# Asking for one packet per load and engine: a packet setting on the row-group loads of a load-bound prefix-sum kernel

## The chip, the cores and the metric

The kernel runs on one core of one Trainium2 chip. The metric is the device time of one execution in microseconds (us), as the median of several runs. The kernel before takes 669.56 us (three runs, 668.67 to 670.19).

## The reference

```python
# x: float32 [4, 4224, 4224]
ps = np.cumsum(np.cumsum(x, axis=1), axis=2)
diag = np.diagonal(ps, axis1=1, axis2=2)
return np.cumsum(diag, axis=1)            # float32 [4, 4224]
```

Every element of `x` counts for some diagonal entry, so all 285 MB have to be read. The rest is adding up.

## The kernel before

A *strip* is six rows for each of the 128 partitions, 768 rows by 4224 columns. It is loaded by one transfer issued from POOL, which casts f32 to bf16 on the way. Three strip buffers rotate. TensorE adds up column groups, VectorE (DVE) and ScalarE add up row parts, and a short chain of small operations ends each of the four batches.

```python
NBUF = 3
strips = ctx.enter_context(tc.tile_pool(name="strips", bufs=NBUF))
...
def strip_tile():
    return strips.tile([P, F2, N], BF16, name="strip")      # 128 x 6 x 4224

def load_rows(o, b, r0):
    f = o.shape[1]
    nc.gpsimd.dma_start(
        out=o, in_=x[b, r0 : r0 + f * P, :].rearrange("(p f) w -> p f w", f=f)
    )

prefetched = []
for i in range(NBUF):
    t = strip_tile()
    load_rows(t, 0, i * F2 * P)
    prefetched.append(t)
...
for b in range(B):
    ...
    for s in range(ns):
        strip = prefetched.pop(0) if prefetched else None
        if strip is None:
            strip = strip_tile()                 # waits until the oldest strip is used up
            load_rows(strip, b, s * F2 * P)
        add_up(strip, F2, s * F2 * P, acc6[:, s], um6)
    ...                                          # a three-row strip, then the batch's end
    nc.sync.dma_start(out=out[b, : j1 * GW]...)  # small stores, on the SP queue
```

The corner of the last batch is loaded by a few smaller transfers that do not go through `load_rows`; the change does not touch them.

Of the kernel before, what the change touches and what calls it, by code (L numbers as in the profile page):

```python
# [17 lines left out]
def kernel(  # L18
# [17 lines left out]
    P = 128  # L36
# [36 lines left out]
    def load_rows(o, b, r0):  # L73
        f = o.shape[1]
        nc.gpsimd.dma_start(  # L75
            out=o, in_=x[b, r0 : r0 + f * P, :].rearrange("(p f) w -> p f w", f=f)
        )

    prefetched = []
# [4 lines that stand above are left out]
# [6 lines left out]
    def upper_mask(f):  # L90
# [20 lines left out]
        out=um1,  # L111
        in_=um1,
# [10 lines left out]
        out=ident,  # L123
        in_=ident,
# [32 lines left out]
    def between_groups(name, turned):  # L157
# [27 lines left out]
        out=weights,  # L185
        in_=weights,
# [61 lines left out]
    for h in range(2):  # L248
        w = GW - h * P
# [3 lines left out]
    for b in range(B):  # L253
# [55 lines left out]
# [3 lines that stand above are left out]
                strip = strip_tile()  # L312
                load_rows(strip, b, s * F2 * P)
            add_up(strip, F2, s * F2 * P, acc6[:, s], um6)
            if not whole and s == 0:
                diag_b = last.tile([P, P], BF16, name="diag_b")
                nc.gpsimd.dma_start(out=diag_b, in_=x[b, TB:N, TB:N])
            if not whole and s == 1:
                row_sums(hs[:, 2:3], diag_b)
                masked(hmu[:, 2, :P], diag_b, um1[:, :P], hu[:, 2:3])  # L320
                nc.vector.tensor_sub(
                    out=tsum[:, 0:1], in0=hs[:, 2:3], in1=hu[:, 2:3]
                )
                for h in range(3):
                    columns(LG, h * P, GW, hmu[:, h, : GW - h * P])
        a6 = acc6[:, :ns]
        sum_up(a6)
        for h in range(2):
# [3 lines left out]
                out=r6[ps, k : k + 2 * ns : 2, :], in_=a6[ps, :, :, 1]  # L332
# [3 lines left out]
        if whole:  # L336
            load_rows(strip[:, :F], b, T0)
            add_up(strip[:, :F], F, T0, acc3[:, 0], um3)
            sum_up(acc3[:, 0])
            nc.vector.tensor_copy(out=r3[:, LG, :], in_=acc3[:, 0, :, 1])  # L340
        else:


            for h in range(2):
                load_rows(strip[:, h * F : h * F + F], b, T0 - (2 - h) * GW)
            add_up(strip[:, :F], F, T0 - 2 * GW, acc3[:, 0], um3)
            sum_up(acc3[:, 0])
            nc.vector.tensor_copy(out=r3[:, row_of(LG - 2), :], in_=acc3[:, 0, :, 1])
            fold_g = psum_s.tile([P, F, 160], FP32, name="fold")
            wp, ws = 1280, 1280 + 1536  # L350
            fold_in(fold_g, strip[:, F:], 0, wp, 160, start=True)
            parts = last.tile([P, F, 4], FP32, name="parts")
            add_up(strip[:, F:], F, T0 - GW, parts, um3, wp, ws)
            nc.vector.tensor_scalar_mul(
                out=parts[:, :, 2], in0=parts[:, :, 2], scalar1=-1.0
            )
            row_sums(parts[:, :, 3], fold_g)
            row_sums(r3[:, row_of(LG - 1), :], parts)
# [37 lines left out]
        for i, src in enumerate((d, c12[:, 0, :])):  # L396
            nc.vector.tensor_tensor_scan(  # L397
                out=c12[:, i, :],
# [8 lines left out]
            out=out[b, : j1 * GW].rearrange("(g i) -> g i", i=GW),  # L407
            in_=c12[t0:NG, 1, :],
# [36 lines left out]
        for fin, c0, c1 in ((fin_a, 0, 2 * P), (fin_b, 2 * P, GW)):  # L445
            nc.vector.tensor_add(
                out=yl[:, c0:c1], in0=fin, in1=c12[0:1, 1, c0:c1]
            )
            nc.sync.dma_start(
                out=out[b, T0 + c0 : T0 + c1].unsqueeze(0), in_=yl[:, c0:c1]  # L450
# [31 lines left out]
```

## Time and profile before

| what | value | where from |
|---|---|---|
| span of the profiled run | 667.0 us | first line of the page |
| DMA engines | nine tenths or more in 39 of 40 slices | slices |
| TensorE / DVE / ScalarE busy | 32% / 50% / 21% | busy times |
| one six-row load, issue to landing | 69.6 us (median) | DMA issues |
| same load, landing to landing | 29.9 us | chain of waits |

The last two rows belong together. A load takes 29.9 us of the engines' time, and the 69.6 us from issue to landing say that it stands in a queue for some 40 us first. A queue that is never empty is what bounds this kernel. The lines themselves are in the prediction.

### The profile page before, as it was taken

To read this page: it belongs to the slowest core of one execution; us is meant where nothing else is said; L and a number is where in the kernel's file an instruction comes from. 1 tells how busy PE (TensorE), PEld (TensorE's weight loads), DVE (VectorE), ACT (ScalarE), POOL (GpSimd) and SP (SyncE) were. 2 spreads that over 40 slices of the span, in tenths; PEclk is the share of its full clock that TensorE was granted. 3 is DMA by queue.
4 is the path that set the end of the run, shared out by engine and by line. 5 is a ranking of instruction groups with operands and counts; after the bars stand their busy time and mean duration, and the time that the engine had idled before them with its cause. 6 is when DMAs were issued, how large, how long until landed. Compare 5 with 4: busy or idle time off the path is not lost.

```text
span 667.0 us, 2828 instructions
## 1 busy us (share of the span) xinstructions
PE 215.1 (32%) x967; PEld 97.2 (15%) x967; DVE 336.3 (50%) x376; ACT 140.1 (21%) x225; POOL 27.0 (4%) x56
## 2 busy tenths in 40 slices
PE   0071522403118254140321633504032254250426
PEld 0030211101003022010110311201011122120202
DVE  2043617366924351745883415266398241635687
ACT  0001120406300103040630020304063002030436
POOL 5000000000000000000000000000000000001000
PEclk9995857666558586665655957567565586765758
DMA  9999999999999999999999999999999999999997
GB/s 203 219 219 219 218 219 219 217 217 216 208 215 219 219 219 217 216 219 219 219 219 215 216 211 217 220 219 216 216 216 219 220 215 218 216 215 219 216 207 144
DMA packets 7384, 143.25 MB, mean 215 GB/s; under 512 B 669, under 2 KB 842, under 8 KB 1866
## 3 DMA queue, kind: packets, MB, share of 16 engines
q0 software_dynamic: 7008, 142.47, 99.7%
q1 hardware_dynamic: 362, 0.61, 0.3%
q8 instruction: 7, 0.11, 0.1%
q14 instruction: 7, 0.06, 0.0%
HBM read 285.47 MB, written 0.07 MB: 428 GB/s over the span
## 4 chain that ended last, share of the span: by engine, by line
another core or an unknown queue 42%; DVE 25%; PE 23%; DMA 5%; issue 4%; DVEq 0%; POOLq 0%
PE d L198 23%; DVE acc L215 17%; DVE mu L218 7%; DMA strip<-in_x_dram 5%; PE fold L198 1%; DVE pu L215 0%; DVE c L397 0%; DVE c L218 0%; DVE tsum L215 0%; DVE acc L301 0%; DVE acc L304 0%; PE carry_ps L198 0%; DVE rows L331 0%; DVEq L218 0%
## 5 line engine op out<-in xcount | busy, mean ns | idle before, releaser
L218 DVE SCALAR_TENSOR_TENSOR mu<-strip,um 128x768 bf16<-128x768 bf16 (+1 forms) x129 | 110.7, 908 | 314.4 <-DMA strip<-in_x_dram 222.3
L198 PE MATMUL d<-strip,sel 128*11 128x384 bf16 x603 | 140.0, 406 | 344.4 <-DMA strip<-in_x_dram 344.4
L210 ACT ACTIVATE dump<-strip 128x416 bf16<-128x416 bf16 (+8 forms) x112 | 128.4, 1146 | 523.2 <-DMA strip<-in_x_dram 520.2
L215 DVE TENSOR_REDUCE acc<-strip 128x6 f32<-128x4608 bf16 (+6 forms) x23 | 195.9, 8518 | 0.0
L198 PEld LDWEIGHTS <-sel 128*11 128x11 bf16 x849 | 86.1, 101 | 526.3 <-issue 488.4
L198 PE MATMUL d<-mu,sel 128*11 128x384 bf16 x243 | 59.7, 355 | 67.5 <-DVE mu L218 67.4
L75 POOL DMA_DIRECT2D strip<-in_x_dram x24 | 16.5, 687 | 555.5 <-DVE acc L215 414.5
L210 ACT ACTIVATION_READ_ACCUMULATOR dump<-strip 128x1 f32 x112 | 20.9, 186 | 0.0
L218 DVE DVE_READ_ACCUMULATOR mu<-strip,um 128x1 f32 x129 | 10.6, 82 | 0.0
L198 PE MATMUL d<-ident,rows 128*11 128x128 f32 x24 | 5.2, 378 | 16.5 <-DVE rows L340 16.5
L198 PE MATMUL fold<-strip,ident_h 128*128 128x480 bf16 (+1 forms) x14 | 4.3, 458 | 8.4 <-DMA strip<-in_x_dram 8.4
L198 PE MATMUL d<-halves,rows 128*11 128x64 f32 x48 | 5.7, 304 | 0.0
L198 PEld LDWEIGHTS d<-halves,rows 128*11 128x11 f32 x48 | 5.1, 136 | 2.1 <-issue 2.1
L198 PEld LDWEIGHTS d<-ident,rows 128*11 128x11 f32 x24 | 2.6, 118 | 18.2 <-DVE rows L340 11.5
L215 DVE TENSOR_REDUCE pu<-d 11x1 f32<-11x384 f32 x4 | 2.2, 546 | 5.5 <-PE d L198 5.5
L397 DVE TENSOR_TENSOR_SCAN c<-ones_row,carry,c 11x384 f32<-11x384 f32 x4 | 4.0, 1006 | 0.1
L397 DVE TENSOR_TENSOR_SCAN c<-ones_row,carry,d 11x384 f32<-11x384 f32 x4 | 4.0, 1001 | 0.1
L198 PEld LDWEIGHTS <-ident_h 128*128 128x128 bf16 x20 | 2.2, 112 | 12.2 <-issue 11.8
L215 DVE TENSOR_REDUCE parts<-strip 128x3 f32<-128x3072 bf16 x1 | 3.4, 3350 | 0.0
L198 PE MATMUL d<-hmu,sel 128*11 128x384 bf16 (+2 forms) x3 | 0.7, 286 | 6.7 <-DVE hmu L218 6.7
L372 POOL DMA_DIRECT2D strip<-in_x_dram x2 | 1.4, 716 | 29.2 <-DVE acc L215 29.2
L215 DVE TENSOR_REDUCE tsum<-strip 128x1 f32<-128x384 bf16 (+2 forms) x3 | 1.7, 568 | 0.9 <-DMA strip<-in_x_dram 0.9
(78 smaller groups left out, 36.0 us busy)
## 6 DMA issues: line engine op xcount, KB each, us to landing
strip<-in_x_dram POOLq DMA_DIRECT2D x19, 6336.0 KB, 69.6
strip<-in_x_dram POOLq DMA_DIRECT2D x5, 3168.0 KB, 55.3
strip<-in_x_dram POOLq DMA_DIRECT2D x1, 1080.0 KB, 45.3
strip<-in_x_dram POOLq DMA_DIRECT2D x1, 768.0 KB, 48.2
head<-in_x_dram SPq DMA_DIRECT2D x1, 528.0 KB, 3.9
strip<-in_x_dram POOLq DMA_DIRECT2D x1, 448.0 KB, 51.1
strip<-in_x_dram POOLq DMA_DIRECT2D x1, 416.0 KB, 49.5
strip<-in_x_dram POOLq DMA_DIRECT2D x1, 160.0 KB, 51.4
```

Source lines behind the costliest of these rows:

```text
L75: nc.gpsimd.dma_start(out=o, in_=x[b, r0 : r0 + f * P, :].rearrange("(p f) w -> p f w", f=f))
L198: nc.tensor.matmul(o, lhsT=lhsT, rhs=rhs, start=start, stop=False, skip_group_check=True)
L210: nc.scalar.activation(out=dump[:, :w], in_=src, func=ACT.Copy, accum_out=acc)
L215: nc.vector.reduce_sum(out=acc, in_=src, axis=AX.X)
L218: nc.vector.scalar_tensor_tensor(out=o, in0=i, scalar=1.0, in1=m, op0=ALU.mult, op1=ALU.mult, accum_out=acc,)
L372: nc.gpsimd.dma_start(out=part_a[:, :, c0:c1], in_=src_a[:, :, c0:c1])
L397: nc.vector.tensor_tensor_scan(out=c12[:, i, :], data0=ones_row, data1=src, initial=carry[:, i : i + 1], op0=ALU.mult, op1=ALU.add,)
```

## The change

The setting asks that all descriptors which one load puts on one DMA engine be one packet. For a six-row load these are 16 (eight partitions, two pieces of 50,688 B read and 25,344 B written each; the trace of before has 5504 such pieces, 16 x 16 for each of 21.5 strips on 16 engines). The hope is for less time between pieces.

```diff
     def load_rows(o, b, r0):
         f = o.shape[1]
         nc.gpsimd.dma_start(
-            out=o, in_=x[b, r0 : r0 + f * P, :].rearrange("(p f) w -> p f w", f=f)
+            out=o,
+            in_=x[b, r0 : r0 + f * P, :].rearrange("(p f) w -> p f w", f=f),
+            single_packet=True,
         )
```

## The prediction

> **What bounds the kernel now.** I read the page's slices first, then its queue table, then the chain of waits, and last the timeline of the engine that issues the loads. The slices and the queue table:
>
> ```profile
> DMA  9999999999999999999999999999999999999997
> GB/s 203 219 219 219 218 219 219 217 217 216 208 215 219 219 219 217 216 219 219 219 219 215 216 211 217 220 219 216 216 216 219 220 215 218 216 215 219 216 207 144
> DMA packets 7384, 143.25 MB, mean 215 GB/s; under 512 B 669, under 2 KB 842, under 8 KB 1866
> q0 software_dynamic: 7008, 142.47, 99.7%
> q1 hardware_dynamic: 362, 0.61, 0.3%
> q8 instruction: 7, 0.11, 0.1%
> q14 instruction: 7, 0.06, 0.0%
> HBM read 285.47 MB, written 0.07 MB: 428 GB/s over the span
> ```
>
> The reader is to see that the 16 DMA engines are full from the first slice to the last, that queue 0 (the strip loads) has nearly all of it, and that the rate is flat. 215 GB/s counts what lands as bf16; the f32 that is read is twice that, 428 GB/s. No compute engine is above 50% busy. The chain of waits has the same at strip level (start, length, what):
>
> ```profile
> 200.07 11.71 PE d L198 x56
> 229.96 10.16 PE d L198 x44
> 259.87 6.93 PE d L198 x32
> 289.75 5.40 PE d L198 x20
> ```
>
> Every strip's matmuls start when its load has landed, and they start 29.89, 29.91 and 29.88 us apart whatever work a strip carries. A six-row load reads 128 x 6 x 4224 x 4 = 12.98 MB; over 29.9 us that is 434 GB/s. The total closes: 19 loads of 6336 KB and 5 of 3168 KB are 21.5 strips, 21.5 x 29.89 = 642.6 us; the first strip starts moving at 34.6 - 29.9 = 4.7 us; the 2904 KB of corner pieces take 2904 / 6336 x 29.9 = 13.7 us; that is 661.0 us. The last piece is consumed from 662.6 us on and the end comes at 667.0, so 1.6 us is left for instruction blocks and the drift of engines, and 4.4 us is the tail after the last byte. **The kernel is one stream of loads** with a short head and tail.
>
> Is the stream ever starved? The issuing engine's timeline:
>
> ```profile
> 53.60 0.78 POOL L75 DMA_DIRECT2D strip<-in_x_dram  x1 [42.81 <-DVE acc L215]
> 84.25 0.71 POOL L75 DMA_DIRECT2D strip<-in_x_dram  x1 [29.87 <-DVE acc L215]
> 145.61 0.70 POOL L75 DMA_DIRECT2D strip<-in_x_dram  x1 [29.95 <-DVE acc L215]
> 174.52 0.72 POOL L75 DMA_DIRECT2D strip<-in_x_dram  x1 [28.21 <-DVE acc L304]
> ```
>
> The load issued at 53.6 us is next only when the third strip has landed, at about 94 us: 40 us in hand. The tightest are those at 145.6 and 174.5 us, whose predecessors land at about 169 and 199 us: some 24 us in hand. So the rings always hold the next load before the last one ends, and a delay of a buffer's release by under 24 us costs nothing.
>
> [...] The trace's records of queue 0 hold 5504 pieces of 25,344 B written (50,688 B read), each some 1886 ns with the next one starting about 1868 ns after (29.89 us / 16): there is no gap between them for a larger packet to close. [...] No view of before shows where packets end[...]. [...] queue 8 has 7 packets of 16 KiB, and they come after 300, 232, 239, 266, 257 and 238 further recorded instructions of TensorE.
>
> **The change part by part.** It removes nothing and adds no instruction: the 24 strip loads keep their bytes, buffers, order and waits. What changes is that the 16 descriptors of a six-row load on one engine (8 partitions, two pieces each; 8 in a three-row load) form one packet.
>
> *Rate inside a load.* 16 pieces at 1868 ns before. [...]
>
> *Between loads.* The completion write behind each load is recorded at 22 ns, and the next load's first piece follows at once: 24 x 22 ns = 0.5 us in all, not changed.
>
> *Issue.* 24 issues of 687 ns on POOL, 16.5 us, all beside the stream with 24 us or more in hand. If building the packet took double, 0.7 us later issue of each, nothing would be seen but in the very first load, some 1 us at most.
>
> *What moves: the other queues wait.* [...] Three users. **The head load** on the SP queue has landed 3.9 us after its issue, about when the first strip's pieces start at 3.7 us; if an engine's share came second, DVE's in-order sum over it would come at about 34 us and put some 2.3 us of DVE work (1.20 + 0.53 + 0.41 + small ones) into the first strip, where 40 us are in hand: 0 us. **The stores** of batches 0 to 2 have no waiter on the path; the last batch's stores are behind loads that the change leaves as they are: 0 us. **Instruction blocks of TensorE** are the one with teeth. When the seven requests were served, TensorE had executed 175, 475, 707, 946, 1212, 1469 and 1707 recorded instructions. [...] Path: 0 us, perhaps 1 or 2 us in one strip of a batch.
>
> Sum: 669.6 [...] = **669.6 us**.
>
> **Rivals.** *Instruction starvation.* The stalls outrun the slack and the rings run dry. For it: [...]DVE depends on TensorE for its buffers (91.9 us of waits for it). Against: 24 to 46 us in hand[...]. If it were to cost 5 us at each of seven blocks: +35 us, 705 us. *A bubble at the packet's end.* If an engine had to finish one packet's writes before it read the next, each of the 24 loads would lose some 1 to 2 us (an estimate: the head load, with next to no data, took 3.9 us from issue to landing): +24 to 48 us, 694 to 718 us. Against: nothing in the trace speaks for it, since the completion record is 22 ns now and the next piece begins at once. *The larger packet is faster.* [...] 668 us. *No effect at all*, the setting does nothing for such large pieces: 669.6 us, not to be told from my main line by the time alone.
>
> **Range and chances.** The main line and two of the four rivals lie between 668 and 671 us; runs of before spread over 1.5 us. The two slow rivals are each given 3 to 4%, and both would be clearly over 2%. [...] Range 667 to 674 us; faster 0.01, within 2% 0.92, slower 0.07.
>
> **What would show it.** Right: the DMA slices still 9 throughout with 219 GB/s in undisturbed ones; strips still 29.8 to 29.9 us apart in the chain; issue to landing for 6336 KB still near 70 us; instruction blocks of queues 8 and 14 now landing only at the end of a load, and idle time of TensorE before matmuls in mid-strip that was not there before. The packet count may stay at 7384 if the records are of descriptors. Wrong: strips more than 30.5 us apart (a bubble, if the same at every strip; starvation, if only at some and with a DMA slice under 9), a queue-0 share under 99%, or pieces recorded at clearly other than 1886 ns.

The sum came to 669.6 us. Two terms are cut from it, 0.5 us less for a faster rate inside a load and 0.5 us more for a short stall of TensorE; both were guesses, and they cancel, so 669.6 us is the time of before. Cut as well is the assumption that with the setting the other queues wait for the rest of a load, up to 29.9 us, where they had waited for one piece of 1.9 us, and what it would do to TensorE: no run shows it. It is tested below as theory B.

## The result, and the profile after

The changed kernel takes 669.88 us (six runs, 669.10 to 672.11) beside 669.67 us of the kernel before. The ratio is 1.0008, with a 95% interval from 0.9992 to 1.0025: the same. (Ratios here are the mean time of one kernel's fast runs over that of the other's of the same rounds, so not quite the ratio of the medians.)

The slices and the queue table of the changed kernel:

```profile
DMA  9999999999999999999999999999999999999997
GB/s 201 219 219 217 217 219 218 217 219 214 211 216 219 219 220 216 218 216 217 219 219 217 217 219 210 220 219 218 219 217 216 216 218 216 219 217 217 215 208 142
DMA packets 7384, 143.25 MB, mean 215 GB/s; under 512 B 669, under 2 KB 842, under 8 KB 1866
q0 software_dynamic: 7008, 142.47, 99.6%
q1 hardware_dynamic: 362, 0.61, 0.3%
q8 instruction: 7, 0.11, 0.1%
q14 instruction: 7, 0.06, 0.0%
HBM read 285.47 MB, written 0.07 MB: 428 GB/s over the span
```

The count of records is the same to the last one, so what the page calls packets are the single pieces, and the page can't show whether they are grouped. Rate and shares are those of before. The chain of waits (start, length, what) and the timeline of the loads' issues:

```profile
201.34 11.51 PE d L200 x56
231.23 9.97 PE d L200 x44
261.14 6.74 PE d L200 x32
291.02 5.21 PE d L200 x20
```

```profile
56.83 0.78 POOL L75 DMA_DIRECT2D strip<-in_x_dram  x1 [46.04 <-DVE acc L217]
85.80 0.71 POOL L75 DMA_DIRECT2D strip<-in_x_dram  x1 [28.19 <-DVE acc L217]
146.69 0.70 POOL L75 DMA_DIRECT2D strip<-in_x_dram  x1 [29.96 <-DVE acc L217]
175.80 0.71 POOL L75 DMA_DIRECT2D strip<-in_x_dram  x1 [28.40 <-DVE acc L306]
```

Strips are again 29.89, 29.91 and 29.88 us apart. All times are 1 to 3 us later than before, because the first strip landed later (its matmuls begin at 36.84 us, not 34.64); that is looked at below. The issue of a load is as short as it was.

Now the one thing that the prediction expected to move, the other queues. The trace has a record with start and length for every piece moved. These lines are taken from those records, not from a view. Queue 8 carries instruction blocks, seven of 16 KiB recorded at 945 ns (median); by their pace they seem to be TensorE's, as from the first to the last there is one for every 255 instructions recorded of it (1707 - 175 = 1532 in six steps). Queue 1 carries the stores:

```
                                            before    after
first block of queue 8 starts at             69.61    71.53 us
  strips land around it at              64.55, 95.37   66.74, 96.65 us
first store of a batch: issued at           188.95   190.23 us
  data pieces start at                192.66-194.04  193.76-195.31 us
  completion writes start at          194.60-195.98  195.70-197.25 us
  the load in progress lands at             200.07   201.34 us
```

With the setting the block still starts in the middle of a load, 4.8 us into it instead of 5.1 us. A store's data and its completion write are on the same engine 1.94 us apart, in both kernels; that is one strip piece (about 1.89 us recorded) and nothing like the rest of a load. None of these waited for the rest of a load. So the time came out as predicted, but the waits did not, and the experiments are about that.

### The profile page after: what moved, and what is told of

It reads as the page before. It is cut to its first block, busy times and chain, and to the rows that moved or that the text cites. A ratio compares the mean times of both kernels' runs of the same rounds, so it can differ in the third digit from the quotient of the medians.

```text
span 667.6 us, 2828 instructions
## 1 busy us (share of the span) xinstructions
PE 211.8 (32%) x967; PEld 96.4 (14%) x967; DVE 336.3 (50%) x376; ACT 140.1 (21%) x225; POOL 26.9 (4%) x56
## 4 chain that ended last, share of the span: by engine, by line
another core or an unknown queue 41%; DVE 27%; PE 22%; DMA 5%; issue 4%; DVEq 0%; POOLq 0%
PE d L200 22%; DVE acc L217 18%; DVE mu L220 7%; DMA strip<-in_x_dram 5%; DVE parts L217 1%; DVE pu L217 0%; DVE c L399 0%; DVE c L220 0%; DVE tsum L217 0%; DVE acc L306 0%; DVE acc L303 0%; PE carry_ps L200 0%; DVE rows L333 0%; DVEq L220 0%
## 5 line engine op out<-in xcount | busy, mean ns | idle before, releaser
L200 PE MATMUL d<-strip,sel 128*11 128x384 bf16 x603 | 137.7, 402 | 346.7 <-DMA strip<-in_x_dram 346.7
```

The source lines that it names most:

```text
L200: nc.tensor.matmul(o, lhsT=lhsT, rhs=rhs, start=start, stop=False, skip_group_check=True)
```

## The experiments

Two theories about the engines, and a third that the setting is idle:

- **A**: an engine takes turns between queues after every piece, whatever the setting says.
- **B**: it drains a whole packet first. The prediction assumed this.
- **Idle**: the setting changes nothing that the engines do, neither turns nor the cost of a piece.

The compiled files decide for Idle: in every pair below that differs in the setting alone they are the same in every byte, while another limit on the size of a piece does change POOL's file. The files that the chip ran were not kept, but nothing in the traces speaks against it. So the two runs of a pair are repeats of one program. They show how engines take turns beside loads as they are compiled; what an engine does with a load that is one packet, they can't show.

### Probes beside the strip loads

Twenty-four tiny loads are put on the SP queue, each waiting for the one before, while strips stream in on queue 0.

```diff
+    probe = last.tile([16, 64], FP32, name="probe")
+    for i in range(24):
+        nc.sync.dma_start(out=probe, in_=x[LB, TB + 16 : TB + 32, 64 * i : 64 * i + 64])
```

Without the setting:

> The kernel before with a chain of 24 small loads on the SP queue (16 partitions, one piece of 256 B for each DMA engine), each waiting for the one before, issued while the first strips are loaded. Theory A (engines take turns between queues after every piece, packet or not) and theory B (turns only at packet boundaries; without the setting a packet is one piece): both expect that a probe waits for at most one strip piece before its data and one before its completion write, 1.9 us each, so 4 to 6 us from probe to probe and all 24 done within about 110 to 150 us. The data-to-completion gap on one engine is 1.94 us, as it is for the stores of the kernel before.

With it:

> The same chain of probes with the one-packet setting on the strip loads. Theory A (turns after every piece whatever the setting): 4 to 6 us from probe to probe, as without it. Theory B (an engine drains a load's 16 pieces before it turns to another queue, as the prediction assumed): each probe waits for the end of a load for its data and perhaps another for its completion, 30 to 60 us from probe to probe, the 24 take over 600 us. I expect A, since the stores and the instruction blocks of the changed kernel already landed in mid-load.

The view of the probe's tile gives the time from issue to landing; first without the setting, then with it:

```profile
DMA to landing us min/median/max: 7.3/7.5/7.5
```

```profile
DMA to landing us min/median/max: 7.3/7.5/7.9
```

The outputs were correct and the times 669.44 and 670.97 us (one run each). No load was drained as a whole: a probe would have taken 30 us or more. This refutes B together with a setting in force, and not B alone, since packets of one piece would look the same. The size was a miss for both theories, 7.5 us instead of 4 to 6: in the run with the setting the second probe's data pieces start 4.6 to 5.2 us after its issue, some two and a half strip pieces and not one. Pieces are only part of it: beside the small pieces of the runs below, 0.07 us each, it is still 3.6 us (median of the probes' pieces, against 4.9 and 5.0 us here). What these 3.6 us are, the runs do not say. The cleanest number is again on one engine. (The records name no engine; data pieces and completion writes of a probe are paired in order of time.) Over the 368 probe pieces issued beside strips, the median from the start of a data piece to that of its completion write is 1893 ns in both kernels: one strip piece.

### The two kernels again, with more rounds

Both were run again with nothing but a comment added.

> The kernel before again (a comment added), as a control: ratio 1.000 within 0.2%. Its profile shows whether the late first strip of the changed kernel (matmuls from 36.8 us instead of 34.6 us) comes by chance: if the theory of chance holds, first strips of the two kernels' repeated profiles spread over 34.5 to 37 us without regard to the setting.

> The changed kernel again (a comment added), with more rounds: theory 'no effect at all' expects a ratio of 0.999 to 1.002 and a first strip that is not always late; theory 'the setting makes the start slower by 2 us' expects a first strip at about 36.8 us again, while the runs without the setting on the same chip start at 34.6 us.

The kernel before against itself gave 1.0001 (interval 0.9986 to 1.0016), the changed one 0.999 (0.9976 to 1.0003), with medians of 670.05 and 669.23 us. With the first result (1.0008) the two comparisons lie on both sides of 1. The difference is under 0.3%, and as the compiled programs are the same, it is the noise between runs of one program.

The late first strip is put to the test by six profiles. The first matmuls of the chain start at:

```
without the setting   34.64  35.67  35.24 us
with the setting      36.84  34.45  36.79 us
```

The earliest of all six has the setting, so it does not always come late. Three profiles each can't exclude a shift of about a microsecond on average, but the times do not show one, and with the same compiled program the setting can't be its cause.

### Smaller pieces, where a packet's cost would count

With 16 large pieces a load, there is no gap between pieces to save (recorded at 1886 ns each, with starts 29.89 us / 16 = 1868 ns apart). So the loads are cut: two rows to a load and a limit on the size of a piece, in two versions that differ only in the setting. The probes ride along.

```diff
-        nc.gpsimd.dma_start(
-            out=o, in_=x[b, r0 : r0 + f * P, :].rearrange("(p f) w -> p f w", f=f)
-        )
+        src = x[b, r0 : r0 + f * P, :].rearrange("(p f) w -> p f w", f=f)
+        for q in range(0, f, 2):
+            nc.gpsimd.dma_start(
+                out=o[:, q : min(q + 2, f), :],
+                in_=src[:, q : min(q + 2, f), :],
+                max_dma_last_dim=1408,
+                single_packet=False,      # True in the other version
+            )
```

> The kernel before with each six-row load cut into three loads of two rows, in pieces of 1408 elements (5.6 KB read, 2.8 KB written; 48 pieces for each engine and load, nine times as many pieces as before), without the one-packet setting, and with the chain of 24 probes. [...] If pieces cost nothing the time stays at 669 to 671 us. Probes: turns after every piece make a probe [...] 2.5 to 4 us.

> The same cut loads with the one-packet setting: 48 pieces in a packet. Theory A1 (the setting takes effect, but engines take turns after every piece): as fast as without it or a little faster [...], probes again 2.5 to 4 us. Theory A2 (the setting has no effect that the chip shows): all numbers within 0.3% of the run without it. Theory B (turns only at packet boundaries): probes wait for packets of 48 x 0.21 = 10 us, 10 to 30 us each.

I had taken the limit for elements; it counts bytes. The pieces read 1408 B and write 704 B, and there are 192 of them on each engine and load. Queue table and rate without the setting, then with it:

```profile
q0 software_dynamic: 200336, 142.47, 131.0%
HBM read 285.57 MB, written 0.07 MB: 401 GB/s over the span
```

```profile
q0 software_dynamic: 200336, 142.47, 131.1%
HBM read 285.57 MB, written 0.07 MB: 401 GB/s over the span
```

The times are 714.09 us without the setting and 714.42 us with it, ratios to the kernel before of 1.0658 and 1.0666. Here pieces do cost something. The trace has 198,144 of them, (198,144 - 5504) / 16 = 12,040 more on each engine than before, and 714.09 - 669.48 = 44.6 us more time: 3.7 ns a piece. (The 43 additional loads' completion writes of 22 ns are 0.9 us of it.) The run with the setting gives none of it back. From data to completion write the probes now take 81 ns in both (a piece is recorded at 74 ns), and 4.1 and 4.2 us from issue to landing. Behind a packet of 192 pieces it would have been some 10 us (an estimate: a third of the 29.9 us of a strip).

The objection is that 192 pieces might be too many for one packet, which no run shows, and that the setting might have been dropped for this reason. The pair was repeated with `max_dma_last_dim=5632`, which makes 48.

> As the run with cut loads, but in pieces of 5632 B read (2816 B written), so that a load has 48 pieces on an engine[...]; no setting. From the run with 1408 B pieces: 44.6 us more for 12,040 more pieces on each engine is 3.7 ns a piece; here 2752 more pieces on each engine: 2752 x 3.7 ns = 10 us, so 680 us.

> The same with the one-packet setting, 48 pieces in a packet. Theory 'the setting gathers pieces into packets, and the 3.7 ns are the packet's': all but 1/48 of the 10 us come back, 670 us, a ratio to its partner of 0.985. Theory 'the setting changes nothing that the engines do': 680 us, ratio within 0.3%, and the data-to-completion gap of the probes is one piece (about 0.22 us) and not a packet (about 10 us).

The times are 682.07 us without and 681.91 us with the setting, ratios of 1.0184 and 1.0179 to the same runs of before (670.07 us). A piece costs (682.07 - 670.07) / 2752 = 4.4 ns, or 4.0 ns without the completion writes, and again nothing of it is saved: with 47 of 48 gone, the time would have been about 670 us. The two cut kernels have the same loads and probes and differ in the pieces alone, so their difference is the cleaner figure: (44.6 - 12.0) us / (12,040 - 2752) = 3.5 ns a piece. That leaves some 2.3 us of each for the 43 additional loads and the probes. From data to completion write it is 236 ns in both, one piece of 229 ns. The one visible difference, 681.0 against 679.0 us of span, is between single profiled runs; the means of all runs do not have it.

### Very small pieces, and loads without a cast

Two more questions, asked with small kernels that only load: does the setting show at the smallest pieces, and is it the cast that keeps it idle? Their outputs are wrong, which doesn't matter for the times.

```diff
+    P, FR, C, M, LAG = 128, 7, 64, 240, 8          # without a cast: 128, 6, 1408, 40, 2
+    for i in range(M + LAG):
+        ...
+            t = pieces.tile([P, FR, C], BF16, name="piece")    # without a cast: FP32
+            nc.gpsimd.dma_start(out=t, in_=x[...], single_packet=False)   # or True
```

> Another kernel, wrong on purpose: 240 loads of 128 partitions by 7 pieces of 512 B read and 256 B written (56 pieces for each engine), no setting, and the probe chain beside them. [...] theory 'the setting works where pieces are small' expects this run to be clearly slower than its partner with the setting. If it is the making of descriptors on POOL that bounds it, both are the same and the DMA share is under 90%.

> The same small loads with the one-packet setting. Theory 'the setting takes effect, our loads were too large to show it': pieces recorded shorter, the 240 loads done 5 to 40% sooner, and the probes' gap between data and completion on an engine a whole packet of 56 pieces (1 us or more) if turns are taken by packet. Theory 'it changes nothing on the chip': piece durations, rate and gaps equal within 1 to 2%.

> Another kernel, wrong on purpose: 40 loads f32 to f32, no cast, 48 pieces of 5632 B for each engine and load, with the one-packet setting and the probe chain beside them. It asks whether the cast is what made the setting idle in all the runs so far. Theory 'the setting works, but not for loads that cast': the probes' data and completion on one engine are a packet of about 48 x 0.21 = 10 us apart, and a probe takes 10 to 30 us. Theory 'engines take turns after every piece with or without it': the gap is one piece, 0.2 to 0.25 us, and a probe takes some 4 us as in the run with pieces of the same 5632 B and a cast (4.3 to 4.5 us).

The two tiny runs took 232.35 and 232.50 us. Their costliest groups, without the setting and with it (time in all, mean ns of one, idle time before):

```profile
L36 POOL DMA_DIRECT2D piece<-in_x_dram x240 | 222.7, 931 | 0.8 <-PEq L76 0.8
```

```profile
L36 POOL DMA_DIRECT2D piece<-in_x_dram x240 | 223.0, 933 | 0.8 <-PEq L76 0.8
```

240 issues of 931 ns fill 223 of 230 us, so POOL's issues bound both, and equal times say nothing about the engines. (The sign that had been expected for this, a DMA share under 90%, did not come: records of pieces overlap, and queue 0 adds up to 187.9% and 187.6%.) (I had also written the pieces at twice their size: they read 256 B and write 128 B.) What counts is inside: the pieces are recorded at 32 ns in both, and from data to completion write the probes take 38 and 34 ns (medians), one piece and not 56 of them (1.8 us).

Without a cast and with the setting, 48 pieces of 5632 B a load:

```profile
DMA to landing us min/median/max: 1.6/4.6/5.2
```

The gap on one engine is 229 ns, with a piece recorded at 220 ns. Here loads land every 10 us, so a whole packet would have been 10 us. So beside these loads, without a cast, an engine turned to the other queue after one piece as well. Whether the cast keeps the setting idle could not be tested in this way: the same kernel compiled with `single_packet=False` gives the same files. No partner of it was run.

### Is the slack what the prediction said?

The prediction leaned on 24 to 46 us in hand at each issue. Since nothing was delayed, the changed kernel never drew on it. The kernel before with two buffers in place of three does.

```diff
-    NBUF = 3
+    NBUF = 2
```

> The kernel before with two strip buffers in place of three, to test the slack that the prediction relied on (24 to 46 us in hand at each issue). One buffer less takes one load time, 29.9 us (15 us behind a three-row load), from each slack: 40 becomes 10, 24.5 becomes 9 to 10, and the tightest, the first strip of the next batch with 24 us, becomes 24 - 29.9 = -6 us. With 2 us from issue to first byte the stream stops for some 8 us once a batch: 3 x 8 = 24 us, perhaps a little more in the last batch: 690 to 705 us. If the slack was misread and the rings run dry at every strip, 21 stops: over 750 us; if the slack was larger than read, 670 us.

It takes 693.57 us, a ratio of 1.0354. Its slices, and the two issues around the end of the first batch:

```profile
DMA  9999999996899999999699999999968999999997
```

```profile
145.59 0.56 POOL L75 DMA_DIRECT2D strip<-in_x_dram  x1 [29.84 <-DVE acc L215]
174.42 0.70 POOL L75 DMA_DIRECT2D strip<-in_x_dram  x1 [28.27 <-DVE acc L304]
```

There is one dent at the end of each of the first three batches. In the records of pieces, engines start no large piece for 8.04 us (from 167.8 us), 8.04 us and 8.03 us, and nowhere else for longer than 2.0 us. Three stops of 8 us are the 24 us that were added. (The 2 us that the expectation allows from issue to first byte: the first load of before is issued at 1.33 us and its first piece starts at 3.73 us, 2.4 us later; here pieces start again 1.4 us after the issue at 174.42 us.) The load issued at 145.59 us is done near 170 us, and the next is only issued at 174.42 us. The slack had been read rightly, place and size.

## Why the prediction was right

The number was right because, by the compiled files, the chip ran the same program twice. The prediction had this only as its rival "no effect at all". Its main line began with "What changes is that the 16 descriptors of a six-row load on one engine ... form one packet", and that premise failed: nothing changed. As far as packets go, the number is right by luck. What it worked out from the trace of before about the bound and the slack holds, and the slack was tested; what it said of packets got no test.

**The bound.** Right. A stream of loads at 434 GB/s ran in both kernels, with strips 29.9 us apart. One term of the closing sum is off: the first strip starts at 3.7 us, as the prediction itself says further down, and not at 4.7. So the sum is 660.0 us, and 2.6 us are left over in place of 1.6; 0.6 us of this is the first strip itself, which takes 30.5 us in the records.

**The rate inside a load.** By adding pieces, 3.5 to 4.4 ns a piece were measured; at 344 pieces an engine that would be 1.2 to 1.5 us (an estimate). The sum hoped for 0.5 us and got none; whether a real packet would give some, no run shows.

**Between loads, and the issue.** Right. The completion writes are recorded at 22 ns and an issue takes 686 ns against 687.

**What moves: the other queues wait.** This step did not happen. It assumed that they wait for the rest of a load. The runs show one piece: 1.89 us, 0.236 us, 0.081 us and some 0.04 us, each with the size of the piece, in programs that are the same with the setting and without it. So neither the delays assumed for TensorE's instructions came, nor the one for the head load, which landed 3.6 us after its issue. Whether they would come behind a real packet stays open. It did no harm to the number, because the prediction had estimated that even the full delay would cost nothing. That last part, that a release may slip by under 24 us, is supported by the run with two buffers; that a delayed instruction block would be harmless was never exercised and was the author's estimate alone.

**The rivals.** Starvation, a bubble at the packet's end (3 to 4% each) and a faster packet were not put to the test, since the setting made no packet: the even strips say nothing about them. "No effect at all" is what came, but not because the pieces are large: the setting was lost before the chip. The prediction said that the time alone could not tell it from the main line, and that the instruction blocks would: they did, against the main line. That they land in mid-load is what the chip shows; that the setting could not have mattered is what the compiled files show.

**What stays open.** What a load that really is one packet would do to the other queues and to the cost of a piece. The records have pieces, not packets, so they can't even tell how many pieces a packet has here.

## What to carry to other kernels

Where a profile shows one stream that keeps the DMA engines busy throughout (here 434 GB/s, nine tenths or more in 39 of 40 slices), look for gaps between its pieces before trying a setting on how that stream is cut. Here the trace of before had none (1886 ns recorded, starts 1868 ns apart), and all 344 pieces on an engine, at the 3.5 to 4.4 ns that one more piece cost in the cut loads, are 1.2 to 1.5 us, about 0.2% (an estimate). Then compare the compiled programs: this takes no run on the chip, and here it would have settled the question first. What can be lost is larger: the same bytes in pieces of 1408 B, in 67 loads in place of 24, cost 6.6%, at about 3.5 ns for every piece more. Before an argument rests on who waits for whom between queues, a chain of tiny probe loads on another queue, and the time from a probe's data to its completion write, measure it in one run.
